# A gated linear unit in float32: four-row groups packed in place in three 64 KiB slots, against two-row tiles with separate outputs

## Chip, cores and metric

One core of one Trainium2 chip runs the kernel. The metric is the device time of one execution, in microseconds (us). The "span" of a profile goes from the first to the last instruction; the reported time is 1.7 to 2.8 us longer.

## The reference

```python
def setup_inputs():
    return {"x": np.random.randn(8192, 8192).astype(np.float32)}

def reference(x):
    a, b = np.split(x, 2, axis=-1)
    return a * (1 / (1 + np.exp(-b)))          # 8192 x 4096, float32
```

So 268.4 MB are read, 134.2 MB are written, and each output needs one sigmoid (ScalarE, "ACT") and one product (VectorE, "DVE").

## The kernel before

A tile is 128 partitions by two rows: a partition loads two whole rows of `x` (64 KiB) and stores two output rows (32 KiB). Two input and two output buffers fill 192 KiB of a partition. Loads go out on the sync queue, stores on the scalar queue.

```python
    pool = ctx.enter_context(tc.tile_pool(name="io", bufs=BUFS))          # BUFS = 2, PAIR = 2
    # ... (a branch for PAIR == 1, not taken)
        x_t = x.rearrange("(n p r) m -> n p (r m)", p=P, r=PAIR)
        out_t = out.rearrange("(n p r) m -> n p (r m)", p=P, r=PAIR)
        # ...
        for i in range(n_tiles):                                          # 32 tiles
            x_sb = pool.tile([P, in_cols], fp32)
            o_sb = pool.tile([P, out_cols], fp32)
            eng(LOAD_ENG, i).dma_start(out=x_sb, in_=x_t[i])              # sync queue
            n_chunks = TAIL_CHUNKS if i >= n_tiles - TAIL_ITERS else 1    # 4 in the last tile
            for r in range(PAIR):
                # ... a_all, b_all, o_all: row r of the tile
                for c in range(n_chunks):
                    # ... a_part, b_part, o_part: chunk c of the row
                    nc.scalar.activation(out=b_part, in_=b_part, func=SIG)
                    nc.vector.tensor_mul(out=o_part, in0=a_part, in1=b_part)
                    if n_chunks > 1:
                        eng(STORE_ENG, i + 1).dma_start(
                            out=out_t[i, :, r * half + lo : r * half + hi], in_=o_part)
            if n_chunks == 1:
                eng(STORE_ENG, i + 1).dma_start(out=out_t[i], in_=o_sb)   # scalar queue
```

Of the kernel before, what the change touches and what calls it, by code (L numbers as in the profile page):

```python
# [2 lines left out]

# [4 lines left out]


@with_exitstack  # L10
def kernel(
    ctx: ExitStack,
    tc: tile.TileContext,
    x: bass.AP,
    out: bass.AP,
):
    nc = tc.nc
    P = nc.NUM_PARTITIONS

    PAIR = int(os.environ.get("GLU_PAIR", "2"))  # L20
    BUFS = int(os.environ.get("GLU_BUFS", "2" if PAIR == 2 else "5"))
    STORE_ENG = os.environ.get("GLU_STORE", "scalar")
    LOAD_ENG = os.environ.get("GLU_LOAD", "sync")
    TAIL_CHUNKS = int(os.environ.get("GLU_TAIL_CHUNKS", "4"))
    TAIL_ITERS = int(os.environ.get("GLU_TAIL_ITERS", "1"))

    n_rows, n_cols = x.shape
    half = n_cols // 2
    assert out.shape == (n_rows, half)

    fp32 = mybir.dt.float32
    SIG = mybir.ActivationFunctionType.Sigmoid

    def eng(name, i):
        if name == "alt":
            name = "sync" if (i % 2 == 0) else "scalar"
        return getattr(nc, name)

    pool = ctx.enter_context(tc.tile_pool(name="io", bufs=BUFS))

    if PAIR == 1:
        x_t = x.rearrange("(n p) m -> n p m", p=P)
        out_t = out.rearrange("(n p) m -> n p m", p=P)
        n_tiles = x_t.shape[0]

        for i in range(n_tiles):
            x_sb = pool.tile([P, n_cols], fp32)
            eng(LOAD_ENG, i).dma_start(out=x_sb, in_=x_t[i])

            n_chunks = TAIL_CHUNKS if i >= n_tiles - TAIL_ITERS else 1  # L50
            csz = half // n_chunks
            for c in range(n_chunks):
                lo = c * csz
                hi = lo + csz
                a_part = x_sb[:, lo:hi]
                b_part = x_sb[:, half + lo : half + hi]
                nc.scalar.activation(out=b_part, in_=b_part, func=SIG)
                nc.vector.tensor_mul(out=a_part, in0=a_part, in1=b_part)
                eng(STORE_ENG, i + 1).dma_start(out=out_t[i, :, lo:hi], in_=a_part)
    else:  # L60
        x_t = x.rearrange("(n p r) m -> n p (r m)", p=P, r=PAIR)
        out_t = out.rearrange("(n p r) m -> n p (r m)", p=P, r=PAIR)
        n_tiles = x_t.shape[0]
        in_cols = PAIR * n_cols
        out_cols = PAIR * half

        for i in range(n_tiles):
            x_sb = pool.tile([P, in_cols], fp32)
            o_sb = pool.tile([P, out_cols], fp32)
            eng(LOAD_ENG, i).dma_start(out=x_sb, in_=x_t[i])  # L70

            n_chunks = TAIL_CHUNKS if i >= n_tiles - TAIL_ITERS else 1
            for r in range(PAIR):
                a_all = x_sb[:, r * n_cols : r * n_cols + half]
                b_all = x_sb[:, r * n_cols + half : (r + 1) * n_cols]
                o_all = o_sb[:, r * half : (r + 1) * half]
                csz = half // n_chunks
                for c in range(n_chunks):
                    lo = c * csz
                    hi = lo + csz  # L80
                    a_part = a_all[:, lo:hi]
                    b_part = b_all[:, lo:hi]
                    o_part = o_all[:, lo:hi]
                    nc.scalar.activation(out=b_part, in_=b_part, func=SIG)  # L84
                    nc.vector.tensor_mul(out=o_part, in0=a_part, in1=b_part)  # L85
                    if n_chunks > 1:
                        eng(STORE_ENG, i + 1).dma_start(  # L87
                            out=out_t[i, :, r * half + lo : r * half + hi], in_=o_part
                        )
            if n_chunks == 1:  # L90
                eng(STORE_ENG, i + 1).dma_start(out=out_t[i], in_=o_sb)


# [1 line left out]
_INS = ['x']  # L95
_OUTS = [((8192, 4096), 'float32')]


# [23 lines left out]
```

## Time and profile before

| | before |
|---|---|
| time, median of the first 3 runs | 936.92 us (936.83 to 936.95) |
| span of the profile | 934.1 us |
| DVE, ACT busy | 30%, 25% |
| both DMA queues together | 99.8% of 16 engines' span |
| rate over the span | 431 GB/s |

These lines are from the page of the kernel before. The DMA line gives the mean busy share of the 16 DMA engines in 40 equal slices, in tenths. The queue lines give packets, bytes and share of the 16 engines' span; q1 is the sync queue (loads), q10 the scalar queue (stores).

```profile
span 934.1 us, 410 instructions
DVE 280.9 (30%) x70; ACT 230.0 (25%) x71; POOL 0.2 (0%) x4
DMA  9999999999999999999999999999999999999998
DMA packets 10226, 402.67 MB, mean 431 GB/s; under 512 B 1136, under 2 KB 1136, under 8 KB 2160
q1 hardware_dynamic: 4608, 268.44, 66.5%
q10 hardware_dynamic: 5616, 134.22, 33.3%
DMA 78%; DVE 15%; ACT 6%; issue 0%; DVEq 0%; ACTq 0%; SPq 0%
```

The last line is the chain of waits. It gives 21% to compute, but the DMA line has no gap: while the chain stands on a compute step of one tile, the engines move the other tile. Here the chain says what released what, not what could be saved.

The table of windows gives, for each stretch of 58 us (two tiles in, two tiles out), busy time of DVE, ACT and POOL, the clock, the DMA share and the rate:

```profile
core 0: us, DVE busy (x) ACT busy (x) POOL busy (x), PEclk, DMA share, GB/s
290.00:348.00 58.00, 17.52 (x4) 14.24 (x4) 0.00 (x0) 1.00 1.00 434
348.00:406.00 58.00, 17.52 (x4) 14.24 (x4) 0.00 (x0) 1.00 1.00 433
406.00:464.00 58.00, 17.52 (x4) 14.25 (x4) 0.00 (x0) 1.00 1.00 433
464.00:522.00 58.00, 17.52 (x4) 14.24 (x4) 0.00 (x0) 1.00 1.00 434
```

The fabric's ceiling of 435.2 GB/s, which the Trainium skill gives (DMA: Bandwidth & Descriptors, "Where 436 GB/s comes from"), is 0.3% to 0.5% above the 433 to 434 GB/s of these stretches. By that figure there is next to nothing left to win without moving fewer bytes.

Below the views, the trace holds a record of every DMA packet: start, duration, size and queue. It doesn't name the engine. Where this document speaks of one engine's sequence, it was put together by joining each packet to the one that ended as it began, so single engines with near-equal times may be swapped; sums over all packets of a queue don't depend on that. "Stretch" is used for the time of a packet over its usual duration (2,418 ns for 64 KiB, 1,213 ns for 32 KiB), summed over all packets and divided by 16 engines. "Gap" is time in which an engine has no packet, averaged over 16. "Ring" stands for the packets that one queue has for one engine, and "completion write" for the 4-byte packet with which each DMA ends on each engine.

### The profile page before, as it was taken

The numbers are of one execution on the slowest core, as the hardware profiler recorded it, in microseconds if no ns is written. First come the engines' busy times: TensorE is split into PE (matmuls) and PEld (weight loads), VectorE is DVE, ScalarE is ACT, GpSimd is POOL, SyncE is SP. The second block draws the span as 40 slices with busy tenths as digits, with TensorE's granted clock in tenths as the row PEclk, the third lists the DMA queues.
The fourth block names the chain that finished last, engine by engine and source line by source line (L and its number), as shares of the span: only waits on it lengthen the run. The fifth ranks groups of instructions, "written<-read, shape, count | busy, mean of one in ns | idle before, by whom it ended". The sixth has DMA issues, their size and how long they took to land.

```text
span 934.1 us, 410 instructions
## 1 busy us (share of the span) xinstructions
DVE 280.9 (30%) x70; ACT 230.0 (25%) x71; POOL 0.2 (0%) x4
## 2 busy tenths in 40 slices
DVE  0333321333213332133321333312333123331234
ACT  0313331133311333113332033320233202333023
POOL 0000000000000000000000000000000000000000
DMA  9999999999999999999999999999999999999998
GB/s 404 404 449 427 427 449 427 427 434 464 404 441 434 428 449 425 451 408 462 410 429 446 425 450 420 453 408 453 421 429 446 424 452 429 441 411 450 424 449 359
DMA packets 10226, 402.67 MB, mean 431 GB/s; under 512 B 1136, under 2 KB 1136, under 8 KB 2160
## 3 DMA queue, kind: packets, MB, share of 16 engines
q1 hardware_dynamic: 4608, 268.44, 66.5%
q10 hardware_dynamic: 5616, 134.22, 33.3%
q14 instruction: 2, 0.02, 0.0%
HBM read 268.44 MB, written 134.22 MB: 431 GB/s over the span
## 4 chain that ended last, share of the span: by engine, by line
DMA 78%; DVE 15%; ACT 6%; issue 0%; DVEq 0%; ACTq 0%; SPq 0%
DMA x_sb<-in_x_dram 78%; DVE o_sb L85 15%; ACT x_sb L84 6%; DVEq L117 0%; ACTq L87 0%; SPq L70 0%; ACTq L84 0%
## 5 line engine op out<-in xcount | busy, mean ns | idle before, releaser
L85 DVE TENSOR_TENSOR o_sb<-x_sb 128x4096 f32<-128x4096 f32 (+1 forms) x70 | 280.9, 4056 | 647.3 <-ACT x_sb L84 647.3
L84 ACT ACTIVATE x_sb<-x_sb 128x4096 f32<-128x4096 f32 (+1 forms) x70 | 228.7, 3315 | 696.1 <-DMA x_sb<-in_x_dram 692.0
L84 ACT ACT_TABLE_LOAD x1 | 1.3, 1283 | 0.7 <-PEq L106 0.7
L106 POOL MEMSET const-bfloat16-1.0<- 128x1 bf16 x1 | 0.1, 102 | 0.0
L106 POOL MEMSET const-uint8-127<- 128x1 uint8 x1 | 0.1, 102 | 0.0
L106 POOL MEMSET const-float32-1.0<- 128x1 f32 x1 | 0.1, 99 | 0.0
L106 POOL MEMSET const-float32-0.0<- 128x1 f32 x1 | 0.1, 98 | 0.2 <-issue 0.2
## 6 DMA issues: line engine op xcount, KB each, us to landing
out_dram<-o_sb ACTq DMA_DIRECT2D x31, 4096.0 KB, 41.8
out_dram<-o_sb ACTq DMA_DIRECT2D x8, 512.0 KB, 6.3
x_sb<-in_x_dram SPq DMA_DIRECT2D x32, 45.5
```

The source lines that it names most:

```text
L84: nc.scalar.activation(out=b_part, in_=b_part, func=SIG)
L85: nc.vector.tensor_mul(out=o_part, in0=a_part, in1=b_part)
L106: nc = _bacc.Bacc("TRN2", target_bir_lowering=False, num_devices=1)
```

## The change

The intent is to spend the same 192 KiB of a partition on three input slots and no output slots. A group is four rows a partition. Rows 0 and 1 land in a "head" slot (two of these), rows 2 and 3 in the one "tail" slot. The products are packed into the head slot in place, and a whole head slot leaves as one store of 64 KiB a partition, contiguous in the output. At the end, the store of group 14 is put behind the last load on the sync queue by hand, so that it runs while the last group is computed.

```diff
-        x_t = x.rearrange("(n p r) m -> n p (r m)", p=P, r=PAIR)
-        out_t = out.rearrange("(n p r) m -> n p (r m)", p=P, r=PAIR)
+    R = 4
+    x_g = x.rearrange("(n p h r) m -> n h p (r m)", p=P, h=2, r=R // 2)
+    out_g = out.rearrange("(n p r) m -> n p (r m)", p=P, r=R)
+    heads = [pool.tile([P, width], fp32, name=f"head{k}") for k in range(2)]
+    tail = pool.tile([P, width], fp32, name="tail")
+
+    def load(g, h):
+        nc.sync.dma_start(out=heads[g % 2] if h == 0 else tail, in_=x_g[g, h])
+
+    def compute(g):
+        head = heads[g % 2]
+        for r in range(R):
+            src = head if r < 2 else tail
+            lo = (r % 2) * n_cols
+            n = 1 if r < 2 else 2                       # rows of the tail by halves
+            w = half // n
+            for c in range(n):
+                a = src[:, lo + c * w : lo + (c + 1) * w]
+                b = src[:, lo + half + c * w : lo + half + (c + 1) * w]
+                o = head[:, r * half + c * w : r * half + (c + 1) * w]
+                nc.scalar.activation(out=b, in_=b, func=SIG)
+                nc.vector.tensor_mul(out=o, in0=a, in1=b)
+
+    def store(g):
+        queue = nc.sync if g == n_groups - 2 else nc.scalar
+        queue.dma_start(out=out_g[g], in_=heads[g % 2])
+
+    load(0, 0)
+    load(0, 1)
+    for g in range(n_groups):                           # 16 groups
+        last_pair = g >= n_groups - 2
+        if g + 1 < n_groups:
+            load(g + 1, 0)
+        compute(g)
+        if g + 1 < n_groups and last_pair:
+            load(g + 1, 1)
+        store(g)
+        if g + 1 < n_groups and not last_pair:
+            load(g + 1, 1)
```

(The removed lines are cut to the two that matter here, and of the added ones the sizes and the pool are left out.)

More of the change, by code (lines that the diff above doesn't have):

```diff
@@ L1 @@
-import os
 from contextlib import ExitStack
@@ L5 @@
 import concourse.tile as tile
-from concourse import bass_utils, mybir
+from concourse import mybir
 from concourse._compat import with_exitstack
@@ L18 @@
     P = nc.NUM_PARTITIONS
-    PAIR = int(os.environ.get("GLU_PAIR", "2"))
-    BUFS = int(os.environ.get("GLU_BUFS", "2" if PAIR == 2 else "5"))
-    STORE_ENG = os.environ.get("GLU_STORE", "scalar")
-    LOAD_ENG = os.environ.get("GLU_LOAD", "sync")
-    TAIL_CHUNKS = int(os.environ.get("GLU_TAIL_CHUNKS", "4"))
-    TAIL_ITERS = int(os.environ.get("GLU_TAIL_ITERS", "1"))
+    fp32 = mybir.dt.float32
+    SIG = mybir.ActivationFunctionType.Sigmoid
     n_rows, n_cols = x.shape
     half = n_cols // 2
-    assert out.shape == (n_rows, half)
@@ L31 @@
-    fp32 = mybir.dt.float32
-    SIG = mybir.ActivationFunctionType.Sigmoid
-    def eng(name, i):
-        if name == "alt":
-            name = "sync" if (i % 2 == 0) else "scalar"
-        return getattr(nc, name)
-    pool = ctx.enter_context(tc.tile_pool(name="io", bufs=BUFS))
-    if PAIR == 1:
-        x_t = x.rearrange("(n p) m -> n p m", p=P)
-        out_t = out.rearrange("(n p) m -> n p m", p=P)
-        n_tiles = x_t.shape[0]
-        for i in range(n_tiles):
-            x_sb = pool.tile([P, n_cols], fp32)
-            eng(LOAD_ENG, i).dma_start(out=x_sb, in_=x_t[i])
-            n_chunks = TAIL_CHUNKS if i >= n_tiles - TAIL_ITERS else 1
-            csz = half // n_chunks
-            for c in range(n_chunks):
-                lo = c * csz
-                hi = lo + csz
-                a_part = x_sb[:, lo:hi]
-                b_part = x_sb[:, half + lo : half + hi]
-                nc.scalar.activation(out=b_part, in_=b_part, func=SIG)
-                nc.vector.tensor_mul(out=a_part, in0=a_part, in1=b_part)
-                eng(STORE_ENG, i + 1).dma_start(out=out_t[i, :, lo:hi], in_=a_part)
-    else:
-        x_t = x.rearrange("(n p r) m -> n p (r m)", p=P, r=PAIR)
-        out_t = out.rearrange("(n p r) m -> n p (r m)", p=P, r=PAIR)
-        n_tiles = x_t.shape[0]
-        in_cols = PAIR * n_cols
-        out_cols = PAIR * half
-        for i in range(n_tiles):
-            x_sb = pool.tile([P, in_cols], fp32)
-            o_sb = pool.tile([P, out_cols], fp32)
-            eng(LOAD_ENG, i).dma_start(out=x_sb, in_=x_t[i])
-            n_chunks = TAIL_CHUNKS if i >= n_tiles - TAIL_ITERS else 1
-            for r in range(PAIR):
-                a_all = x_sb[:, r * n_cols : r * n_cols + half]
-                b_all = x_sb[:, r * n_cols + half : (r + 1) * n_cols]
-                o_all = o_sb[:, r * half : (r + 1) * half]
-                csz = half // n_chunks
-                for c in range(n_chunks):
-                    lo = c * csz
-                    hi = lo + csz
-                    a_part = a_all[:, lo:hi]
-                    b_part = b_all[:, lo:hi]
-                    o_part = o_all[:, lo:hi]
-                    nc.scalar.activation(out=b_part, in_=b_part, func=SIG)
-                    nc.vector.tensor_mul(out=o_part, in0=a_part, in1=b_part)
-                    if n_chunks > 1:
-                        eng(STORE_ENG, i + 1).dma_start(
-                            out=out_t[i, :, r * half + lo : r * half + hi], in_=o_part
-                        )
-            if n_chunks == 1:
-                eng(STORE_ENG, i + 1).dma_start(out=out_t[i], in_=o_sb)
@@ new lines @@
+    R = 4
+    n_groups = n_rows // (P * R)
+    x_g = x.rearrange("(n p h r) m -> n h p (r m)", p=P, h=2, r=R // 2)
+    out_g = out.rearrange("(n p r) m -> n p (r m)", p=P, r=R)
+    width = 2 * n_cols
+    pool = ctx.enter_context(tc.tile_pool(name="slots", bufs=1))
+    heads = [pool.tile([P, width], fp32, name=f"head{k}") for k in range(2)]
+    tail = pool.tile([P, width], fp32, name="tail")
+    def load(g, h):
+        nc.sync.dma_start(out=heads[g % 2] if h == 0 else tail, in_=x_g[g, h])
```

## The prediction

> **What bounds the kernel now.** The 16 DMA engines, nearly without a gap. In the table of windows, every stretch of 58 us from 116 to 870 us (two tiles: 16.78 MB in, 8.39 MB out) has a DMA share of 1.00 and 433 to 434 GB/s. The queue table puts 99.8% of the 16 engines' span on the two queues. The Trainium skill (DMA: Bandwidth & Descriptors, "Where 436 GB/s comes from") gives 435.2 GB/s as the fabric's ceiling; the trace agrees to 0.3%. DVE is busy 30%, ACT 25%. The chain of waits names DMA for 78% and compute for 21%, but during those compute steps the DMA engines work on the other tile, so that 21% is not to be won.
>
> The trace's packet records show what is left. A 64 KiB load packet takes 2,418 ns and the next starts some 4 ns before it ends: 2.414 us a packet; a 32 KiB store packet 1,213 ns (1.209 from start to start); a 4 KiB packet of the last tile 159 ns. From 2.7 us, when all 16 engines have a packet, to about 932 us all idle time sums to less than 0.5 us. The span is 934.1; the reported time 2.8 us more.
>
> **What the change does.** The bytes stay, and so do the load packets (4,096 of 64 KiB). Each engine's 248 store packets of 32 KiB and 64 of 4 KiB become 128 of 64 KiB. If a 64 KiB store costs what a 64 KiB load does, that is 309.0 us for 299.8 + 9.9: 0.7 us less. Fewer completion writes save about 0.15 us. I expect about 1 us in all.
>
> **Does the new order leave gaps?** Estimate from the durations: after the tail slot lands, ACT starts 0.45 us later; half rows of 2,048 cost about 1.90 us on ACT and 2.29 us on DVE, so the last product ends 0.45 + 1.90 + 4 x 2.29 = 11.5 us after the landing, and the store's first packet comes about 1 us later, at the sixth packet boundary. The next head load (8 packets an engine, 19.3 us) covers that with two packets to spare. Then 8 store packets alternate with 7 or 8 loads; at the store's end about 3 packets (7 us) of the tail load are left, against about 2 us to land, issue the next head load and start it. So the engines never run dry; a group takes 24 packets, about 58 us. At the end, the store of group 14 (19.3 us) covers the last 12.7 us of compute.
>
> **Prediction:** 935.9 us, 8 in 10 between 934.3 and 938.5. Faster by over 2%: 1%. Within 2%: 96%. Slower by over 2%: 3%.
>
> **What would show it right.** Windows of 58 us still at 434 GB/s and share 1.00; about 6,900 packets for 10,226; 64 KiB store packets at 2,418 ns; about 11 us from ACT's first tail op to DVE's last; DVE busy rises to about 288 us and ACT to about 238 with no effect; median store landing near 39 us.
>
> **What would make it wrong.** (a) Gaps: if the store's landing and the next issue take over 7 us, each of some 14 groups loses the excess; windows would drop under 434. (b) 64 KiB writes to HBM slower than 32 KiB ones: store packets over 2,430 ns. (c) Engines drifting apart, so that one runs dry while others work. (d) A longer ragged end: an idle stretch before the last store.

## The result, and the profile after

The changed kernel takes 953.47 us (median of 4 runs, 947.49 to 955.23), the kernel before 936.88 us. The ratio is 1.0165 (95% interval 1.0134 to 1.0197). A ratio in this document is the mean time of one kernel's runs over that of the other's of the same rounds, so it isn't quite the ratio of the medians quoted. The time lies outside the predicted range (934.3 to 938.5), on the slow side.

The profile is of the fastest of the four runs (947.49 us). Its page answers line for line to the one above:

```profile
span 945.4 us, 379 instructions
DVE 283.9 (30%) x96; ACT 232.2 (25%) x97; POOL 0.2 (0%) x4
DMA  9999999999999999999999999999999999999998
DMA packets 6914, 402.67 MB, mean 426 GB/s; under 512 B 768, under 2 KB 768, under 8 KB 768
q1 hardware_dynamic: 4752, 276.83, 68.9%
q10 hardware_dynamic: 2160, 125.83, 30.7%
DMA 78%; DVE 15%; ACT 3%; DVEq 0%; issue 0%; SPq 0%; ACTq 0%
```

The windows, with the same columns as above:

```profile
core 0: us, DVE busy (x) ACT busy (x) POOL busy (x), PEclk, DMA share, GB/s
290.00:348.00 58.00, 15.98 (x6) 14.43 (x6) 0.00 (x0) 1.00 0.99 420
348.00:406.00 58.00, 16.60 (x6) 14.43 (x6) 0.00 (x0) 1.00 1.00 427
406.00:464.00 58.00, 17.27 (x7) 14.43 (x6) 0.00 (x0) 1.00 1.00 428
464.00:522.00 58.00, 17.45 (x7) 14.28 (x6) 0.00 (x0) 1.00 1.01 432
```

This is the reading that matters most. The DMA share is still 0.99 to 1.01, but the rate is 420 to 432 GB/s. The engines are as busy as before and move less: packets take longer. A busy share can't show this. The Trainium skill warns of the busy share for another reason (Perfetto Trace Analysis, "Identifying the Most-Contended Engine": for DMA, use HBM utilization instead of occupancy, because with 16 engines occupancy misleads); its advice holds for this trace, with a share of 0.99 to 1.01 at 420 to 432 GB/s.

The packet records say which packets:

| | before | changed |
|---|---|---|
| load packets of 64 KiB: count, mean ns | 4,096, 2,425 | 4,096 loads + 128 of the store on the sync queue, 2,465 |
| store packets of the scalar queue: bytes, mean ns | 32 KiB, 1,213 | 64 KiB, 2,418 (every one) |
| stretch on the sync queue | 1.8 us | 12.3 us |
| gaps, 5 to 920 us | under 0.1 us | 1.1 us |

The stores cost what was predicted, 2,418 ns each. The loads don't. The sum comes out: 10.5 us more stretch, 1.0 us more gaps, 0.6 us more at a more ragged end, 0.1 us more before the first packets, and 1.0 us less for fewer packets and completion writes, 11.3 us in all (before rounding), against 945.4 - 934.1 = 11.3 us measured.

Where the stretch sits shows in the sequence of one engine (put together from the packet records; start in us, L for load, S for store, bytes, ns; 4-byte completion writes left out):

```
changed kernel                      kernel before
109.72 L 65536 2418                 641.79 S 32768 1213
112.13 L 65536 2441                 643.00 L 65536 2418
114.57 L 65536 3481   <- 1.06 over  645.41 S 32768 1213
118.05 S 65536 2418                 646.62 L 65536 2418
120.46 L 65536 2418                 649.04 L 65536 2418
122.88 S 65536 2418                 651.45 S 32768 1213
125.30 S 65536 2418                 652.67 S 32768 1213
127.71 L 65536 2418                 653.88 L 65536 2418
```

In the changed kernel a group's store starts after a stretch of loads alone, and it's the load packet ahead of the first store packet that is long (in this group on 9 of the 16 engines by over 0.1 us). In the kernel before the two kinds alternate all the time, because stores get one 32 KiB packet per 64 KiB load packet: the store of a tile then takes as long as the load of one and the store ring never runs empty once it's filled. Sorted by what follows on the same engine:

| load packets of 64 KiB followed by | before: count, mean stretch | changed: count, mean stretch |
|---|---|---|
| a store, with another store close before (alternating) | 3,360, 0 ns | 1,353, 6 ns |
| a store, the first after loads alone | 16, 958 ns | 240, 456 ns |
| a load | 720, 17 ns | 2,631, 30 ns |

The kernel before pays for this turn once on each engine (at 38.7 us, its very first store), the changed kernel 14 times: 6.9 of its 12.3 us of stretch. (Its 15th burst, the last store, follows the store of group 14 in the other ring and not loads; the 16 packets ahead of it have no stretch and stand among the 240. Without them the mean is 489 ns.) Of the rest, 3.4 us and a gap of 1.0 us fall on the third to fifth load packets after a store burst, which is where a head load begins.

The timeline shows why there (start us, us, engine, line, what; SPq is the sync queue, ACTq the scalar queue):

```profile
112.83 0.33 SPq L43 DMA_DIRECT2D tail<-in_x_dram  x1
112.83 0.36 ACTq L61 DMA_DIRECT2D out_dram<-head  x1
...
156.22 0.33 SPq L43 DMA_DIRECT2D head<-in_x_dram  x1
```

The store is issued at 112.83, but its first packets come at 117.1 to 119.6, after the packet in flight and one more load packet; the prediction had taken 1 us and the next packet boundary. So the store's burst ends one packet later, with two load packets left instead of three. The next head load can be issued only at 156.22, and the last engine gets its completion write of the tail load at 160.7. One engine ran dry for 1.15 us at 158.2.

### The profile page after: what moved, and what is told of

Its sections match the earlier page's. It is cut to its first block, busy times and chain, and to the rows that moved or that the text cites. A ratio compares the mean times of both kernels' runs of the same rounds, so it can differ in the third digit from the quotient of the medians.

```text
span 945.4 us, 379 instructions
## 1 busy us (share of the span) xinstructions
DVE 283.9 (30%) x96; ACT 232.2 (25%) x97; POOL 0.2 (0%) x4
## 2 busy tenths in 40 slices
DMA packets 6914, 402.67 MB, mean 426 GB/s; under 512 B 768, under 2 KB 768, under 8 KB 768
## 4 chain that ended last, share of the span: by engine, by line
DMA 78%; DVE 15%; ACT 3%; DVEq 0%; issue 0%; SPq 0%; ACTq 0%
DMA tail<-in_x_dram 78%; DVE head L57 15%; ACT tail L56 3%; DVEq L100 0%; SPq L43 0%; ACTq L56 0%
## 5 line engine op out<-in xcount | busy, mean ns | idle before, releaser
L57 DVE TENSOR_TENSOR head<-tail 128x2048 f32<-128x2048 f32 x64 | 142.3, 2285 | 337.4 <-ACT tail L56 337.4
L57 DVE TENSOR_TENSOR head<-head 128x4096 f32<-128x4096 f32 x32 | 141.6, 4425 | 295.6 <-ACT head L56 293.9
L56 ACT ACTIVATE tail<-tail 128x2048 f32<-128x2048 f32 x64 | 116.9, 1897 | 394.0 <-DMA tail<-in_x_dram 394.0
L56 ACT ACTIVATE head<-head 128x4096 f32<-128x4096 f32 x32 | 114.0, 3608 | 286.5 <-DMA head<-in_x_dram 286.5
## 6 DMA issues: line engine op xcount, KB each, us to landing
out_dram<-head ACTq DMA_DIRECT2D x15, 43.4
```

The source lines that it names most:

```text
L56: nc.scalar.activation(out=b, in_=b, func=SIG)
L57: nc.vector.tensor_mul(out=o, in0=a, in1=b)
```

## The experiments

The first theory, START: a load packet is stretched whenever a DMA has to start on a ring that has run empty or nearly so. Its rivals: PITCH (reads of 64 KiB out of every 128 KiB are slow) and SIZE (64 KiB stores disturb loads). After the tenth run START had to be narrowed to TURN.

| run | time, median us | ratio to before, 95% | stretch in its profile |
|---|---|---|---|
| e1, contiguous loads | 955.58 | 1.0187 (1.0154 to 1.0219) | 18.6 us |
| e2, before with the pitch | 937.04 | 1.0001 (0.9986 to 1.0016) | 2.2 us |
| e3, one queue | 951.16 | 1.0154 (1.0137 to 1.0171) | 4.2 us |
| e4, split store | 941.41 | 1.0049 (1.0034 to 1.0064) | 2.2 us |
| e5, one queue, end kept | 938.49 | 1.0016 (1.0003 to 1.0030) | 3.5 us |
| e6, split store, end mended | 936.33 | 0.9993 (0.9981 to 1.0006) | 2.1 us |
| e7, before with small loads | 954.75 | 1.0179 (1.0139 to 1.0220) | 11.5 us (8.4 loads, 3.1 stores) |
| e8, changed kernel again | 954.33 | 1.0211 (1.0174 to 1.0248) | 19.0 us |
| e9, extra start, 8 packets | 990.84 | 1.0575 (1.0542 to 1.0608) | 27.6 us |
| e10, tiny store on a busy ring | 948.92 | 1.0127 (1.0072 to 1.0181) | 14.3 us |
| e11, changed kernel, control | 953.59 | 1.0184 (1.0159 to 1.0210) | 15.8 us |
| e12, extra start, 1 packet | 953.29 | 1.0177 (1.0160 to 1.0194) | 17.7 us |

The kernel before took 936.3 to 937.0 us (medians) beside them. e1 to e4 ran in one call on one chip, and so did e5 to e8 and e9 to e11; e12 ran alone.

### e1: contiguous loads (PITCH taken away)

```diff
-    x_g = x.rearrange("(n p h r) m -> n h p (r m)", p=P, h=2, r=R // 2)
+    x_g = x.rearrange("(n h p r) m -> n h p (r m)", p=P, h=2, r=R // 2)
```

> The changed kernel with one line edited: each half load now reads one contiguous 8 MiB block (a row pitch of 64 KiB from partition to partition) in place of 64 KiB out of every 128 KiB. Order, sizes, queues and waits stay; the rows come out permuted, so the result is wrong on purpose. Theory START (a load packet is stretched whenever a DMA has to start on a ring that has run empty or nearly so: each store, and each head load): nothing changes, 947 to 955 us, about 0.45 us over 2,418 ns on the last load packet ahead of each first store packet. Theory PITCH (the 128 KiB pitch of the reads makes load packets slow): back to 935 to 938 us, no load packets over 2,450 ns beyond the first.

955.58 us. Its output is wrong, which doesn't matter for the time. Nothing got better, so the 128 KiB pitch isn't the cause. The first store packets of a burst again have stretched loads ahead of them, 817 ns on average (240 packets). That is more than in the first profile of the changed kernel, which was of its fastest run.

### e2: the kernel before with that pitch

```diff
-        x_t = x.rearrange("(n p r) m -> n p (r m)", p=P, r=PAIR)
+        x_t = x.rearrange("(n p h r) m -> n h p (r m)", p=P, h=2, r=PAIR)
```

(`out_t` alike, and `[i // 2, i % 2]` for `[i]`.)

> The kernel before, with the rows dealt to tiles so that its loads read 64 KiB out of every 128 KiB and its stores write 32 KiB out of every 64 KiB; correct result, same order and waits. START: 936 to 938 us, since its store ring never runs empty. PITCH: 945 us or more, with some hundred load packets over 2,450 ns.

937.04 us, correct, ratio 1.0001. PITCH falls from this side too.

### e3 and e5: all stores in the loads' ring

```diff
 # e3
-        queue = nc.sync if g == n_groups - 2 else nc.scalar
+        queue = nc.sync
 # ... and store(g) ahead of load(g + 1, 1) in every group
```

> The changed kernel with every store on the sync queue, and each store issued ahead of the next tail load. Loads and stores then stand in one ring behind each other: store, tail load, head load, 8 packets each, and a DMA is issued with several packets still ahead of it. 64 KiB packets and the 128 KiB pitch stay. START: the stretched packets before stores (6.9 us in sum) and at the head loads (3.4 us of stretch and 1.1 us of gaps) go, and the time falls to 935 to 938 us. PITCH: still 945 us or more. A third theory, SIZE (64 KiB writes disturb reads): still 945 or more too.

951.16 us: a miss in time, but not through stretch. The stretch fell to 4.2 us (3.6 without the very first load packets, the figure in the next text) and the windows inside are at 434 GB/s. The last 37 us hold the loss (same columns as above, of this run):

```profile
406.00:464.00 58.00, 17.75 (x6) 14.43 (x6) 0.00 (x0) 1.00 1.00 434
464.00:522.00 58.00, 17.75 (x6) 14.43 (x6) 0.00 (x0) 1.00 1.00 434
912.00:929.00 17.00, 8.90 (x4) 7.31 (x4) 0.00 (x0) 1.00 0.21 89
```

The edit had put the store of group 14 ahead of the last load too, so nothing was left to move while the last tail was computed: about 15 us of gap. That is exactly what the hand-made order at the end avoids. The expectation had overlooked it. e5 keeps that end and differs from the changed kernel in one line:

```diff
 # e5
-        queue = nc.sync if g == n_groups - 2 else nc.scalar
+        queue = nc.scalar if g == n_groups - 1 else nc.sync
```

> The run before this one with all stores on the sync queue lost 15 us to one gap at its end, because the store of group 14 stood ahead of the last load and nothing covered the last compute; its stretch was only 3.6 us. Here the stores of groups 0 to 13 go to the sync queue, ahead of the next tail load, and the end is the changed kernel's own: last load, then the store of group 14, and the last store on the scalar queue. One line differs from the changed kernel. 64 KiB packets, pitch, slots and waits on slots stay. START: about 936 us (935 to 938), stretch of the packets ahead of the first store packets under 3 us in sum, no idle gaps inside. SIZE (64 KiB stores disturb loads, whatever the ring): 947 to 955 as before.

938.49 us, half a microsecond over START's range of 935 to 938 and far from SIZE's, with 64 KiB stores, the pitch, the slots and the bytes all kept. The windows are back:

```profile
290.00:348.00 58.00, 17.75 (x6) 14.44 (x6) 0.00 (x0) 1.00 1.00 435
348.00:406.00 58.00, 17.75 (x6) 14.43 (x6) 0.00 (x0) 1.00 1.00 432
406.00:464.00 58.00, 17.75 (x6) 14.44 (x6) 0.00 (x0) 1.00 1.00 434
464.00:522.00 58.00, 17.75 (x6) 14.43 (x6) 0.00 (x0) 1.00 1.00 432
```

SIZE falls. One line, the queue of 14 stores, takes away some 16 us (954.33 against 938.49 us). Loads alone still turn to stores here, 14 times, but behind each other in one ring; 1.8 us of the 3.5 us of stretch is the very first load packets and the very first store, and the other stores together have at most the remaining 1.7. The queues now stand behind each other, so head loads are also issued well ahead, and gaps inside are under 0.1 us: this run takes away both losses and doesn't tell one from the other. What is left over the kernel before is mostly the end: the engines finish over 4.1 us (931.5 to 935.6), in the kernel before over 1.1.

That spread is telling. The completion writes of a DMA lie 4.1 us apart (median) in this run and 2.4 us in the changed kernel. So engines drifting apart, which the prediction had named as a danger, isn't by itself what costs time.

### e4 and e6: stores cut in two

```diff
 # e4
-        queue = nc.sync if g == n_groups - 2 else nc.scalar
-        queue.dma_start(out=out_g[g], in_=heads[g % 2])
+        part = slice(h * n_cols, (h + 1) * n_cols)
+        nc.scalar.dma_start(out=out_g[g][:, part], in_=heads[g % 2][:, part])
 # called for h = 0 after rows 0 and 1, for h = 1 after rows 2 and 3
```

> The changed kernel with each store cut in two: rows 0 and 1 (32 KiB a partition) go out as soon as they are computed, rows 2 and 3 after the tail, all on the scalar queue. Stores are then spread over the group and alternate with loads nearly all the time, as in the kernel before; the pitch of the loads stays. START: few starts on an empty ring, 936 to 939 us. PITCH: 945 us or more. SIZE: 936 to 939 as well, since store packets are 32 KiB again.

941.41 us, 2 us over the range. The stretch is gone (2.2 us, as in the kernel before; loads ahead of a first store packet after loads alone: only the 16 of the very first store), and again it is the end that was overlooked: from 922 to 928.5 us the DMA engines wait for the last products.

```diff
 # e6, beside e4's
                 nc.vector.tensor_mul(out=o, in0=a, in1=b)
+                if g == n_groups - 1 and r >= 2:
+                    part = slice(r * half + c * w, r * half + (c + 1) * w)
+                    nc.sync.dma_start(out=out_g[g][:, part], in_=o)
 # and e4's store of rows 2 and 3 is left out for the last group
```

> The kernel with each store cut in two, 941.4 us, had an idle gap of 6 us at its end (922 to 928.5 us of the trace) and next to no stretch. Here the last group's rows 2 and 3 go out by half rows of 8 KiB a partition on the sync queue as they are computed. If that gap is all that was wrong with it, 935 to 936.5 us, equal to or a shade under the kernel before; any other result says that something else was lost too.

936.33 us against 937.03 us, ratio 0.9993 with an interval that includes 1. So the new slots are sound, if stores flow all the time. It isn't shown to be faster than the kernel before, and no other run was.

### e7: the kernel before, made to have bursts

```diff
-            eng(LOAD_ENG, i).dma_start(out=x_sb, in_=x_t[i])
+            for r in range(PAIR):
+                row = slice(r * n_cols, (r + 1) * n_cols)
+                eng(LOAD_ENG, i).dma_start(out=x_sb[:, row], in_=x_t[i][:, row])
```

> The kernel before with each load issued as two DMAs of one row (32 KiB a partition) each, on the same queue, nothing else changed. Load and store packets are now of one size, so an engine that alternates between the rings gives stores half of its time, not a third: a store should be done in about 20 us of each 29, and the store ring runs empty between stores, as in the changed kernel, though stores stay at 32 KiB and the order of the work is the same. START: some 31 starts on an empty ring at 0.4 to 0.8 us each, so 948 to 960 us, with the stretched load packets just ahead of each first store packet. SIZE or PITCH: 937 to 939 us (256 more packets on each engine cost about 1 us).

954.75 us. Load packets of 32 KiB give the stores half of an engine's time while the two alternate, not a third; a store lands 23.9 us after its issue (median; 41.8 before), and stretches of loads alone appear. The old kernel now loses as much as the changed one, with no byte, slot or order of work changed. Not all of it is stretch, though. Of the 20 us of span, 9.7 us are stretch and 1.6 us gaps inside; about 7 us are gaps at the end, because the stores have no backlog left to cover the last tile's compute, and 1.2 us go to the larger number of packets (of the four stretches of 58 us from 290 us on, the first line below is the slowest; the others have 431 to 432 GB/s):

```profile
406.00:464.00 58.00, 17.70 (x4) 14.47 (x4) 0.00 (x0) 1.00 1.00 425
936.00:948.00 12.00, 3.43 (x3) 4.00 (x4) 0.00 (x0) 1.00 0.51 208
```

So stretched load packets ahead of the bursts appear as START had it (498 packets, mean 202 ns, 6.3 us in sum), but even with all 9.7 us its 31 starts cost some 0.3 us each, less than the 0.4 to 0.8 expected, and the time was right partly by luck. Some 3 us of this stretch lie on store packets, which in the changed kernel have next to none.

### e8 and e11: the changed kernel again

No edit.

> The changed kernel once more beside the others, as a control: 947 to 955 us. Its first profile came from its fastest run; this one should show more stretch if the run is slower (START says that the spread of its times is spread of the stretch).

> The changed kernel, as the same-chip control of the two: 950 to 962 us.

954.33 us (953.55 to 962.16; one run above the range) and 953.59 us. Three profiles of the changed kernel now have spans of 945.4, 948.9 and 952.2 us and a stretch of 12.3, 15.8 and 19.0 us: in these three, the spread of its times is the spread of its stretch. The load packet ahead of a burst's first store packet has 456, 772 and 801 ns over.

### e9, e10 and e12: extra starts on the store ring

```diff
 # e9
                 nc.scalar.activation(out=b, in_=b, func=SIG)
+                if r == 2 and c == 0 and g + 1 < n_groups:
+                    nc.scalar.dma_start(out=out_g[g + 1][:, :128], in_=b[:, :128])
 # e10: in_=head[:, :128]     (goes out before the tail lands, behind the previous store)
 # e12: out_g[g + 1][:16, :128], in_=b[:16, :128]
```

> The changed kernel plus one tiny store a group on the scalar queue (512 B a partition, 64 KiB in all[...]), issued some 2.5 to 4 us after the tail lands, when the store ring has run empty; it writes sigmoid values into rows that the next group's store overwrites, so the result stays correct. It is done before the real store is issued, so each group now has two starts on an empty ring for one. START: 5 to 13 us slower than the changed kernel of the same call, with stretched load packets around the tiny stores too. If the stretch is paid once for each stretch of loads (or by the bytes stored), no more than 1 us slower.

990.84 us. Far off both expectations, and the design was at fault. While both rings have packets, an engine in these records serves one of a ring and then one of the other, whatever their sizes (completion writes count as packets); the tiny store had 8 packets of 512 B on each engine, so up to 8 load packets of 2.4 us went by before the real store's first. It landed 21.6 us after its issue. It reads the tail slot, so the next tail load had to wait for that landing as well (one was issued at 368.84 us, 12.6 us after the real store at 356.22), and the late store made the next head load late: 29 us of gaps in sum, 24 of them from 5 to 920 us (the text of e12 has 22). What it does tell: the load packets ahead of the real store's first packet are still stretched (240, mean 948 ns), although tiny packets stood in its ring, and those ahead of the first tiny packet, on an empty ring, are not (240, mean 7 ns).

> Its control: the same number of tiny stores of the same size on the same queue, but issued right after the head's products, while the previous group's store still fills the store ring, so they start on a ring that is busy. Correct result for the same reason. START: the time of the changed kernel of the same call plus 0 to 1 us. If it is the number of DMAs that costs, as slow as the run with tiny stores on the empty ring.

948.92 us (941.47 to 953.85) beside the control's 953.59: the number of DMAs isn't a cost. It shows the same thing as e9 in passing. The tiny packets now fill much of the loads-only time, and no load packet ahead of a tiny one is stretched (926 of them, mean 0 ns), while those ahead of the first 64 KiB store packet are (240, mean 663 ns).

That contradicts START as stated: a DMA that starts on an empty ring isn't the cause. TURN took its place: the cost belongs to the turn from loads alone to loads alternating with large stores of the other ring. e12 puts them against each other, with one tiny packet an engine:

> The run with an extra start on an empty ring (990.8 us) mended. There each tiny store had 8 packets of 512 B an engine, and an engine served one of them per 64 KiB load packet, so the tiny store held the ring for 20 us and the real store behind it came late (22 us of gaps in sum). Here it covers 16 partitions, one packet of 512 B an engine, at the same place: on an empty ring, between the tail's landing and the real store. Correct result. START, the theory that every start on an empty ring costs about 0.5 to 0.9 us: 959 us or more, stretched load packets before the tiny packets too. TURN, its successor: the cost belongs to the turn from loads alone to loads alternating with large stores, and a tiny store neither pays nor spares it: the changed kernel's 947 to 956 us again, with the load packets ahead of the tiny ones within 50 ns of 2,418 on average and the stretch still just ahead of the first 64 KiB store packet.

953.29 us. TURN holds and START falls. One engine of e12 (not itself stretched in this group; start in us, as above) shows where the tiny packet stands:

```
220.97 L 65536 2418
223.39 L 65536 2418
225.80 S 512 27          <- extra start, ring empty before and after
225.83 L 65536 2418
228.25 L 65536 2418
230.66 L 65536 2418      <- the place of the stretch, where there is one
233.07 S 65536 2418
```

| load packets followed by | e10 | e12 | e11 (control) |
|---|---|---|---|
| a tiny store | 926, 0 ns | 236, 6 ns | none |
| the first large store of a burst | 240, 663 ns | 240, 715 ns | 240, 772 ns |
| a large store, alternating | 1,355, 14 ns | 1,351, 16 ns | 1,355, 6 ns |

(count, mean stretch)

## Why the prediction was wrong

- **Right: what bounds the kernel.** The DMA engines do, before and after; compute (DVE 30%, ACT 25%) is off the path in both, but for the late head loads below.
- **Right: the store packets.** Predicted 2,418 ns for 64 KiB, measured 2,418. About 1 us of saving was there, and was buried. Packet count (6,914), DVE (283.9 us for "about 288") and ACT (232.2 for "about 238") came out or nearly so.
- **Wrong, and decisive: "The bytes stay, and so do the load packets".** The sum took every load packet at the 2.414 us of the old steady state, in which loads and stores always alternate. The new schedule has 14 stretches of loads alone on each engine, and the turn to stores costs the load packet ahead 0.49 to 0.86 us on average (0.46 to 0.80 when the last burst is counted too, as in the tables). That term was taken as zero; it measured 6.9 us in the first profile, 11.6 and 12.0 us in the other two. The old trace had it once, at 38.7 us: 16 load packets of 3.4 us ahead of the first store. The packet records were at hand for the prediction, and it didn't look at the packets that differed from the usual duration.
- **Wrong: "at the store's end about 3 packets (7 us) of the tail load are left ... So the engines never run dry".** Two packets were left (4.8 us): a store's first packet starts 4.0 to 6.8 us after its issue (the middle 90% over engines and stores, median 5.3) and not at the next boundary, and the engines finish a store 2.5 us apart. The head load starts late or just in time, which cost 1.0 us of gaps and some 3.4 us of stretch in the first profile. Median landing of a store: 43.4 us for "near 39".
- **Named dangers:** (a), gaps, was real but small; (b), slow 64 KiB writes, didn't happen; (c), drift, happened (2.4 us) but is larger in e5, which is fast; (d), a ragged end, 0.6 us. The danger that decided wasn't on the list. "Windows would drop under 434" was named as the sign of gaps; they dropped at a DMA share of 1.00.

Shown: neither the pitch (e1, e2) nor the size of the stores (e5, e7), nor the number of DMAs (e10), nor a start on an empty ring (e12) is the cause; keeping stores flowing (e4, e6) or putting them into the loads' ring (e5) removes the loss; bursts put into the old kernel bring it in (e7).

Open: why the turn costs anything. No record says what the engine does in the extra microsecond, nor why a turn inside one ring is nearly free after the first, nor what makes the same turn cost 489 ns in one run and 858 ns in another. Within one run it varies more: in the first profile the turn at 59 us costs 1,088 ns (mean over the engines), the one at 708 us 908 ns and the one at 590 us 14 ns. How closely the engines turn together doesn't explain it (first store packets within 1.9 us at 708, within 1.6 us at 590). And e5 doesn't separate the turn from the late head loads: their split is read from the packet records, not from a run.

## What to carry to other kernels

In a kernel bound by its DMA engines, look at the rate beside the busy share: a share of 1.00 at 424 (e8, 116 to 870 us) instead of 434 GB/s means stretched packets, and the packet records say which. Keep loads and stores of two rings mixed all the time, or put them into one ring, rather than storing in large bursts after loads alone; the ratio of the packet sizes bears on whether they stay mixed (loads of 64 KiB with stores of 32 KiB did, loads of 32 KiB with the same stores, e7, didn't). When stores or slots are reordered, ask at the end of the kernel what still moves while the last piece is computed: three of these runs (e3, e4, e7) lost 6 to 15 us there.

## What the Trainium skill lacked or had wrong

- DMA: Bandwidth & Descriptors, "Issuing engines are not separate DMA queues", says that issuing from several engines only saves sequencer time. Bandwidth agrees where packets aren't stretched (433 to 434 GB/s with two rings in the kernel before, 432 to 435 with one in e5), but the queue of 14 stores alone made 954.33 or 938.49 us. The page lacks the cost of the turn from loads alone to large stores in the other ring: 0.49 to 0.86 us for each engine and turn, on average.
- The same page, "Queues, rings and completion order", says that an engine takes the rings in turn by packets of some 9 to 17 descriptors. In these runs it was one packet record at a time: one 64 KiB load, then one store packet of 64 KiB, 32 KiB or 512 B (how many descriptors a record holds isn't shown). It lacks the consequence: a store of 64 KiB in all (8 packets of 512 B an engine) takes 21.6 us to land beside 64 KiB loads.
- No page has how late a DMA's first packet comes on a loaded engine: 4.0 to 6.8 us after the issue here (median 5.3), with 64 KiB packets in the other ring.
- Perfetto Trace Analysis, "Identifying the Most-Contended Engine", warns of DMA occupancy. It lacks that packets themselves can take longer, so that the same share goes with different rates: a share of 0.99 to 1.01 at 420 to 435 GB/s in the windows above.
